# Second expert layer: 24 of 32 experts in the order of their rows, with 32 slots each, four at a time

## The chip, the cores and the metric

The kernel runs on one core of a Trainium2 chip. The metric is the device time of one execution in microseconds (us); each time given for a kernel is the median of several runs. The profile is of one execution.

## The reference

Two transformer blocks work one after the other on 256 tokens of width 1024; each ends in a mixture of experts. The change lies in the second one, `hier_moe`, in 32-bit floats:

```python
def hier_moe(h, w_rg, b_rg, w_re, b_re, w1e, w3e, w2e):
    t = h.reshape(-1, d)                                   # 256 x 1024
    pg = softmax(t @ w_rg + b_rg)                          # 4 groups
    pg_top, g_idx = top_k(pg, 1)
    le = (t @ w_re + b_re).reshape(-1, 4, 8)               # 8 experts of each group
    le_sel = take_along_axis(le, g_idx[:, :, None], axis=1)[:, 0]
    pe_top, e_idx = top_k(softmax(le_sel), 2)
    wts = pg_top * pe_top / sum(pe_top)
    cw = ...                                               # 256 x 32, two weights in each row
    for e in range(32):
        he = silu(t @ w1e[e]) * (t @ w3e[e])               # 1024 -> 256
        out = out + cw[:, e:e + 1] * (he @ w2e[e])         # 256 -> 1024
    return out
```

Each token goes to two experts of one group, so 512 rows are spread over 32 experts, 16 for each on average, and unevenly. The expert layer of the first block has 32 experts too, with larger weights and four experts for each token.

## The kernel before, in words

`Ker.run` calls four stages: `block1`, `moe1` (first expert layer), `block2`, `moe2` (second expert layer, the end of the kernel). A scheduler places each instruction on its engine's queue, by the order of the program and by what is ready at that point; an engine then works its queue in order.

In `moe2` every expert has 64 slots. `slots` ranks the tokens of each expert with matrix products and gives `pm`, the slot of each token in each expert (-1 where it isn't routed there), and the counts. `onehots` (L1152) makes the selection matrices `oh` of four experts, `gather` (L1207) multiplies the tokens with them, so that `g` holds the 256 slots of four experts side by side, and hands out its steps as a generator that `first2` draws from. `first2` (L1435) takes two experts: for gate weights `w1e` and then up weights `w3e`, eight steps of 128 rows, both experts in turn, each with 64 of the 128 columns of the array (L1445, tile `ab`). `second2` (L1453) is a generator in three parts: transposes (L1456, L1458) and the requests for the down weights `w2e`; down products (L1471, tile `y`) and their weighting by the router (`weighted`, L1176 and L1177); and eight products that add the rows back to the tokens (L1478, tile `sum`). `step2` moves each pending `second2` one part further; it is called between the gate and the up products of `first2` and after it. So the down products of a pair come after the up products of the pair behind it, and their weights are fetched before the up weights of that pair.

Weights come in tiles of 1 MB (`wload`, L302), all on SP's DMA queue: three tiles for each expert, 96 in all. They go round 13 buffers, five from the pool `wp` that all stages share (`own`) and eight from a pool of this stage (`ahead`); `fetch` asks for the next one, and the first eight tiles are asked for at the start of the stage, in the eight.

After the last expert stands `overflow` (L1226): it loads the largest count into a register of each engine (L1231), and only if an expert has more than 64 rows (L1232) it runs a loop with further slots. In `moe1` the same test stands after expert 11 of 32 (`OVF`); ahead of it the pending work is finished and the next nine tiles are requested, in the buffers of the stage's own pools alone. At the end of `moe2` the sums are gated and added to `x` (L1506, L1507), normed and stored.

The modulation rows (`modrow`, L358, tile `modps`) are products with 32 stationary columns, four side by side in the array.

Of the kernel before, what the change touches and what calls it, by code (L numbers as in the profile page):

```python
# [15 lines left out]
PSUM = bass.MemoryType.PSUM  # L16

# [3 lines left out]
OVF = 11  # L21
MODS1 = [(1, j) for j in range(4, 12)] + [(2, j) for j in range(12)]
# [50 lines left out]
def shape_consts():  # L73
    c = {}
    ident = np.eye(128, dtype=np.float32)
    perm = np.zeros((128, 128), np.float32)
    for m in range(128):
        b, r = divmod(m, 64)
        perm[b * 64 + (r + 32) % 64, m] = 1.0
    tri = (np.arange(128)[:, None] < np.arange(128)[None, :]).astype(np.float32)  # L80
    n_freq = 16
    inv = (np.float32(10000.0) ** (-np.arange(n_freq, dtype=np.float32) / np.float32(n_freq))).astype(np.float32)
    row = np.repeat(np.arange(4), 64).astype(np.float32)
    col = np.tile(np.arange(64), 4).astype(np.float32)
# [6 lines left out]
    c['fconst'] = np.ascontiguousarray(np.concatenate([ident, fold, tri, iota, perm, cosT, sinT], 1))  # L91
# [139 lines left out]
class Ker:  # L231
# [296 lines left out]
    def block1(self, p, late, xtile):  # L528
# [24 lines left out]
        nc.sync.dma_start(rc, d['fconst'][:, 544:])  # L553
# [427 lines left out]
        ys = {}  # L981
# [150 lines left out]
    def slots(self, p, sel):  # L1132
# [12 lines left out]
        cnt = p.tile([128, 33], I32, name="cnt")  # L1145
        nc.vector.tensor_copy(cnt[:, 0:32], ps[:, 64:96])
        mx = self.sm.tile([128, 1], F32, name="cmax")
        nc.vector.reduce_max(mx, ps[:, 64:96], axis=AX.X)
        nc.vector.tensor_copy(cnt[:, 32:33], mx)  # L1149
        return pm, cnt  # L1150

    def onehots(self, p, pm, e0):  # L1152

        nc = self.nc
        oh = p.tile([128, 2, 4, 64], F32R, name="oh", tag="oh", bufs=2)
        for b in range(2):
            nc.vector.tensor_tensor(oh[:, b], self.iota[:, None, 0:64].to_broadcast([128, 4, 64]),
                                    pm[:, b, e0:e0 + 4, None].to_broadcast([128, 4, 64]), op=OP.is_equal)
        return oh
# [66 lines left out]
    def overflow(self, p, cnt, pm, cw, xs, A, B, expert, gbufs=1):  # L1226
# [4 lines left out]
        most = nc.values_load(cnt[0:1, 32:33], min_val=0, max_val=256)  # L1231
        with tc.If(most > 64):  # L1232
            with tc.For_i(0, 32) as i:
                n = nc.values_load(cnt[0:1, bass.ds(i, 1)], min_val=0, max_val=256)
                with tc.If(n > 64):
# [3 lines left out]
                    for r in range(1, 4):  # L1239
# [9 lines left out]
                        expert(g, 0, i, ohv, w)  # L1249
# [48 lines left out]
    def moe1(self, p, route, ahead, spare):  # L1298
# [24 lines left out]
        pm, cnt = self.slots(p, sel)  # L1323
# [19 lines left out]
        for e in range(32):  # L1343
# [19 lines left out]
            if e == OVF:  # L1363
# [4 lines left out]
                self.overflow(p, cnt, pm, cw, xs, A, B, late)  # L1368
# [3 lines left out]
    def moe2(self, p, route, ahead):  # L1372
# [8 lines left out]
        def fetch(n, e, slot=None):  # L1381
            if isinstance(e, int) and (n, e) in first:
                return first.pop((n, e))
            return self.wload(src(n, e), slot=slot)
        first = {}
        first = {k: fetch(*k, ahead) for k in [(n, e) for e0 in (0, 2) for n in ('w1e', 'w3e', 'w2e') for e in (e0, e0 + 1)][:NW2B]}
        self.wi = 0

        gs = self.rp.tile([128, 1024], F32, name="gsb", tag="gf")
# [7 lines left out]
        pm, cnt = self.slots(p, sel)  # L1397
# [37 lines left out]
        def first2(g, c0, e0, feed):  # L1435
            ps = self.ps("ab")
            for i, n in enumerate(('w1e', 'w3e')):
                if i:
                    step2()
                w = [fetch(n, e0 + j).rearrange("p (k n) -> p k n", k=8) for j in range(2)]  # L1440
# [12 lines left out]
        def second2(act, e0, oh, wv):  # L1453
# [3 lines left out]
            for b in range(2):  # L1457
                nc.tensor.transpose(pt[:, 256 + 128 * b:384 + 128 * b],  # L1458
                                    oh[:, b, e0 % 4:e0 % 4 + 2, :].bitcast(F32).rearrange("p e s -> p (e s)"), self.ident)
# [4 lines left out]
            w2 = [fetch('w2e', e0 + j) for j in range(2)]  # L1464
            yield
            ys = []
            for s in range(2):
                y = self.ps("y")
                for k in range(2):
                    for j in range(2):  # L1470
                        nc.tensor.matmul(y[64 * j:64 * j + 64, :], aT[:, 128 * k + 64 * j:128 * k + 64 * j + 64],  # L1471
# [3 lines left out]
            for b in range(2):  # L1475
                for s in range(2):
                    for i in range(2):
                        nc.tensor.matmul(sums[b][s], oT[:, 128 * b:128 * b + 128], ys[s][i], start=(e0 + i == 0), stop=(e0 + i == 31))  # L1478

        for e in range(0, 32, 2):  # L1480
            if e % 4 == 0:
                oh = self.onehots(p, pm, e)
                g, feed = self.gather(p, xs, 4, [oh[:, b].rearrange("p e s -> p (e s)") for b in range(2)], A, B, 2)
                next(feed)
            if e == 16:
                self.bcast_rows([(3, 2), (3, 3)], [gs[:, c] for c in cs],
                                lambda o, ps: nc.vector.scalar_tensor_tensor(o, ps, 1.0, o, op0=OP.add, op1=OP.mult))
            act = first2(g, 64 * (e % 4), e, feed)
            if e == 0:
                cw = cw()  # L1490
            if e % 4 == 0:
                sw = self.slot_weights(p, [(slice(64 * (j % 2), 64 * (j % 2) + 64), j // 2, [oh[:, b, j, :] for b in range(2)],
                                            [cw[:, b, e + j:e + j + 1] for b in range(2)]) for j in range(4)], "sw", 2)
            step2()
            pend.append(second2(act, e, oh, sw[:, e // 2 % 2:e // 2 % 2 + 1]))
        while pend:
            step2()
        self.overflow(p, cnt, pm, cw, xs, A, B, late, 2)
# [631 lines left out]
```

## Time and profile before

| | |
|---|---|
| time, median of 3 runs | 2146.15 us (2144.57 to 2146.51) |
| time of the profiled execution | 2146.77 us |
| its span, first to last instruction | 2144.9 us |
| PE busy in the span | 2007.6 us (94%) |
| mean granted TensorE clock | 0.970 of full |
| moved by DMA | 646.08 MB, 301 GB/s on the mean |
| second expert layer, first gather to last sum | 1842 to 2123 us |

PE is TensorE's matrix products, PEld its weight loads, DVE VectorE, ACT ScalarE, POOL GpSimd, SP SyncE, whose queue issues the weight transfers; a "q" behind an engine's name means its sequencer. Products on PE are pipelined and their ends are modelled, so that a busy PE isn't PE at its peak. A line like L1445 is a line of the kernel, `out<-in` the tiles written and read, `128*64 128x512` a product with 64 stationary columns and 512 moving ones. Each 32-bit product shows as two instructions; products of tiles split into a high and a low part show as one. In brackets stands the idle time before an instruction, and what ended it.

### The profile page before, as it was taken

The page shows a single profiled execution, that of the slowest core. Times are in us where ns is not written, and L with a number is a line of the kernel's source. Part 1 is how long each engine was busy: PE and PEld are TensorE (multiplying, and loading weights), DVE is VectorE, ACT ScalarE, POOL GpSimd, SP SyncE. Part 2 cuts the span into 40 slices and gives each one's busy share as a digit, 9 for nine tenths or more (in the row PEclk, how much of TensorE's full clock was granted, in tenths as well). Part 3 has the DMA queues.
Part 4 walks back from the last instruction along what each step waited for, and adds up shares of the span by engine and source line. Part 5 has one row for each costly group of instructions (what it writes and reads, how often), then busy time and mean ns, then how long its engine had stood idle before and what let it go on. Part 6 is the DMA issues. An engine that isn't in the chain of part 4 may idle for free. (4 is left out here: it accounts for less than half of the span.)

```text
span 2144.9 us, 30936 instructions
## 1 busy us (share of the span) xinstructions
PE 2007.6 (94%) x13008; PEld 1172.9 (55%) x13009; DVE 918.6 (43%) x1766; ACT 529.8 (25%) x927; POOL 63.2 (3%) x66
## 2 busy tenths in 40 slices
PE   5999999999899999989999999999789998899995
PEld 3788888877633333333333333333268997665552
DVE  5766664454323332332423333333477654322223
ACT  3434463444300000000000000010244634312112
POOL 0000000000000000000000000000033101000000
PEclk9999999999999999989999999999899998999998
DMA  9254637622899999889999999999662232799980
GB/s 356 83 228 184 234 128 282 247 90 82 325 426 427 412 427 417 366 360 405 427 427 427 426 427 427 426 427 427 243 239 105 100 135 105 316 387 381 358 337 26
DMA packets 95127, 646.08 MB, mean 301 GB/s; under 512 B 11524, under 2 KB 12548, under 8 KB 19076
## 3 DMA queue, kind: packets, MB, share of 16 engines
q1 hardware_dynamic: 93296, 642.79, 74.0%
q8 instruction: 107, 1.75, 0.3%
q10 hardware_dynamic: 1684, 1.21, 0.2%
q14 instruction: 40, 0.33, 0.0%
HBM read 642.91 MB, written 1.05 MB: 300 GB/s over the span
## 5 line engine op out<-in xcount | busy, mean ns | idle before, releaser
L1262 PE MATMUL gu<-w,gT 128*64 128x512 f32 x2048 | 480.9, 596 | 0.0
L1262 PEld LDWEIGHTS gu<-w,gT 128*64 128x64 f32 x2048 | 148.1, 137 | 277.7 <-issue 255.8
L1293 PE MATMUL y<-w,aT 128*64 128x512 f32 x1024 | 231.0, 604 | 0.4
L487 DVE TENSOR_TENSOR wsl<-w,wsh 128x1024 fp32r<-128x1024 f32 (+1 forms) x141 | 168.5, 1205 | 98.5 <-ACT wsh L486 98.3
L486 ACT CAST wsh<-w 128x1024 fp32r<-128x1024 f32 (+1 forms) x141 | 143.4, 1030 | 167.0 <-PE tp L500 109.2
L1272 DVE TENSOR_SCALAR act<-gu 128x256 f32<-128x256 f32 x64 | 27.2, 424 | 307.2 <-PE gu L1332 303.9
L1177 DVE SCALAR_TENSOR_TENSOR ylo<-y,sw,yhi 128x512 fp32r<-128x512 f32 x64 | 48.1, 751 | 254.7 <-ACT yhi L1176 254.7
L1293 PEld LDWEIGHTS y<-w,aT 128*64 128x64 f32 x1024 | 72.5, 140 | 149.7 <-issue 143.4
L499 PE MATMUL tp<-hs,wsh 128*128 128x256 f32 (+1 forms) x424 | 140.2, 331 | 0.0
L501 PE MATMUL tp<-hs,wsl 128*128 128x256 f32 (+1 forms) x424 | 134.9, 318 | 4.1 <-DVE wsl L487 4.1
L500 PE MATMUL tp<-hs,wsh 128*128 128x256 f32 (+1 forms) x424 | 134.2, 317 | 0.0
L1445 PE MATMUL ab<-w,gT 128*64 128x256 f32 x1024 | 128.0, 383 | 0.1
L1176 ACT ACTIVATE yhi<-y,sw 128x512 fp32r<-128x512 f32 x64 | 44.0, 687 | 294.9 <-PE y L1332 241.9
L1193 DVE TENSOR_TENSOR gated<-co,gtb 128x512 f32<-128x512 f32 x128 | 88.3, 690 | 34.9 <-PE co L1188 27.4
L1274 ACT ACTIVATE sge<-act 128x512 f32<-128x512 f32 x32 | 20.2, 630 | 331.3 <-DVE act L1272 331.3
L1445 PEld LDWEIGHTS ab<-w,gT 128*64 128x64 f32 x1024 | 77.9, 137 | 39.6 <-issue 10.7
L499 PEld LDWEIGHTS tp<-hs,wsh 128*128 128x128 f32 x424 | 82.4, 194 | 16.3 <-issue 4.9
L1218 PE MATMUL ga<-oh,xhi 128*128 128x256 f32 x256 | 75.8, 325 | 15.9 <-DVE cnt L1149 6.9
L1194 DVE TENSOR_TENSOR x<-x,gated 128x512 f32<-128x512 f32 x128 | 88.2, 689 | 3.3
L501 PEld LDWEIGHTS tp<-hs,wsl 128*128 128x128 f32 x424 | 82.2, 194 | 9.8 <-DVE wsl L487 4.7
L499 PE MATMUL tp<-hi,wsh 128*128 128x256 f32 x288 | 85.5, 297 | 0.0
L500 PEld LDWEIGHTS tp<-hs,wsh 128*128 128x128 f32 x424 | 82.3, 194 | 4.5 <-issue 0.7
(548 smaller groups left out, 3242.1 us busy)
## 6 DMA issues: line engine op xcount, KB each, us to landing
w<-in_wgu_dram SPq DMA_DIRECT2D x256, 1024.0 KB, 13.4
w<-in_wdn_dram SPq DMA_DIRECT2D x128, 1024.0 KB, 14.1
w<-in_win_dram SPq DMA_DIRECT2D x50, 1024.0 KB, 5.8
w<-in_w3e_dram SPq DMA_DIRECT2D x32, 1024.0 KB, 8.8
w<-in_w1e_dram SPq DMA_DIRECT2D x32, 1024.0 KB, 9.2
w<-in_w2e_dram SPq DMA_DIRECT2D x32, 1024.0 KB, 7.6
w<-in_wada_dram SPq DMA_DIRECT2D x24, 1024.0 KB, 6.0
w<-in_wmod_dram SPq DMA_DIRECT2D x16, 1024.0 KB, 5.7
```

The lines of the kernel that those rows point to most:

```text
L486: nc.scalar.copy(hi, src)
L487: nc.vector.tensor_sub(lo, src, hi.bitcast(F32))
L499: nc.tensor.matmul(out, a[0], b[0], start=first, stop=False)
L500: nc.tensor.matmul(out, a[0], b[1], start=False, stop=False)
L501: nc.tensor.matmul(out, a[1], b[0], start=False, stop=last)
L1177: nc.vector.scalar_tensor_tensor(lo, y, w, hi.bitcast(F32), op0=OP.mult, op1=OP.subtract)
L1193: nc.vector.tensor_mul(part, o[s], gate[:, cs])
L1194: nc.vector.tensor_add(x[:, b, cs], x[:, b, cs], part)
L1218: nc.tensor.matmul(ps[:, 256 * kk:256 * kk + 64 * n], xs[i][:, b, 128 * (k + kk):128 * (k + kk) + 128], ohv[b], start=(b + i == 0), stop=( ...
L1262: nc.tensor.matmul(gu[j][64 * s:64 * s + 64, :], g[:, k, c0:c0 + 64], w[:, 1024 * s + 512 * j:1024 * s + 512 * j + 512], start=(k == 0), s ...
L1293: nc.tensor.matmul(y[64 * s:64 * s + 64, :], aT[:, k % 4, k // 4, :], w[:, o:o + 512], start=(k == 0), stop=False)
L1445: nc.tensor.matmul(ps[64 * j:64 * j + 64, 256 * i:256 * i + 256], g[:, k, c0 + 64 * j:c0 + 64 * j + 64], w[j][:, k, :], start=(k == 0), st ...
```

## The change

The experts of `moe2` get places. Experts 0 to 3 keep theirs (`FIXED`); the other 28 are sorted by their number of rows, most first, on the chip (`sorted_places`): a key from the count, a comparison of all keys with each other, a permutation matrix `perm`, and the table `inv` of the expert at each place. `by_place` permutes the slots and the router weights (`pmP`, `cwP`) with transposes and products.

Places 0 to 7 (`WIDE`) have 64 slots and go two at a time as before; places 8 to 31 have 32 slots and go four at a time, each with 32 of the 128 columns, and a gather serves eight experts instead of four. From place 4 on SP loads the expert's number from `inv` into a register (`place`), and the address of its weights is worked out from it. The order of requests, the 13 buffers and the number of tiles stay.

The overflow test, which now asks whether a count exceeds the slots of its place, moves from the end of the stage to the point behind place 15: the pending halves are finished there, and eight tiles (gate and up weights of places 16 to 19) are requested in the stage's own eight buffers. `moe1` gets the new form of the test with its 64 slots. The table `fconst` grows by 97 columns, which ACT's queue loads at the start of `moe2`.

```diff
+FIXED, WIDE = 4, 8
...
+    off = np.zeros((128, 97), np.float32)
+    e = np.arange(32)
+    off[:, 0:32] = np.where(e < FIXED, 32768 * (FIXED - e), -e)
+    off[0:32, 32] = off[0, 0:32]
+    off[:, 33:65] = np.where(e < WIDE, 64, 32)
+    off[0:32, 65:97] = e[:, None]
+    c['fconst'] = np.ascontiguousarray(np.concatenate([ident, fold, tri, iota, off, perm, cosT, sinT], 1))
...
+    def excess(self, p, over):
+        nc = self.nc
+        exc = p.tile([128, 33], I32, name="exc")
+        nc.vector.tensor_copy(exc[:, 0:32], over)
         mx = self.sm.tile([128, 1], F32, name="cmax")
+        nc.vector.reduce_max(mx, over, axis=AX.X)
+        nc.vector.tensor_copy(exc[:, 32:33], mx)
+        return exc
+
+    def sorted_places(self, p, sel, pm, count, off):
         nc = self.nc
+        keyrow, keycol, self.caps, ecol = off[:, 0:32], off[0:32, 32:33], off[:, 33:65], off[0:32, 65:97]
+        key = p.tile([128, 32], F32, name="key")
+        nc.vector.scalar_tensor_tensor(key, count, 64.0, keyrow, op0=OP.mult, op1=OP.add)
+        pc = self.ps("kc")
+            nc.tensor.matmul(pc[0:32, 0:1], sel[:, b, :], self.ones[:, 0:1], start=(b == 0), stop=(b == 1))
+        kcol = p.tile([32, 2], F32, name="kcol")
+        nc.vector.scalar_tensor_tensor(kcol[:, 0:1], pc[0:32, 0:1], 64.0, keycol, op0=OP.mult, op1=OP.add)
+        gt = p.tile([32, 64], F32, name="gt")
+        nc.vector.tensor_scalar(gt[:, 0:32], key[0:32, :], kcol[:, 0:1], None, op0=OP.is_gt)
+        nc.vector.reduce_sum(kcol[:, 1:2], gt[:, 0:32], axis=AX.X)
+        perm = gt[:, 32:64]
+        nc.vector.tensor_scalar(perm, self.iota[0:32, 0:32], kcol[:, 1:2], None, op0=OP.is_equal)
+        pi = self.ps("inv")
+        nc.tensor.matmul(pi[0:32, 0:32], ecol, perm, start=True, stop=True)
+        inv = p.tile([32, 32], I32, name="inv")
+        nc.vector.tensor_copy(inv, pi[0:32, 0:32])
+        pmP = self.by_place(p, pm, perm, "pmP")
+        cc = p.tile([32, 128], F32, name="cc")
+        nc.vector.tensor_copy(cc, pc[0:32, 0:1].to_broadcast([32, 128]))
+        po = self.ps("cp")
+        nc.tensor.matmul(po[:, 0:32], cc, perm, start=True, stop=True)
+        over = p.tile([128, 32], F32, name="over")
+        nc.vector.tensor_sub(over, po[:, 0:32], self.caps)
+        return perm, inv, pmP, self.excess(p, over)
+
+    def by_place(self, p, t, perm, name):
+        nc = self.nc
+        pt = self.ps("plT")
+        for b in range(2):
+            nc.tensor.transpose(pt[0:32, 128 * b:128 * b + 128], t[:, b, :], self.ident)
+        tT = p.tile([32, 256], F32, name="plT")
+        nc.scalar.copy(tT, pt[0:32, 0:256])
+        po = self.ps("pl")
+        for b in range(2):
+            nc.tensor.matmul(po[:, 32 * b:32 * b + 32], tT[:, 128 * b:128 * b + 128], perm, start=True, stop=True)
+        o = p.tile([128, 2, 32], F32, name=name)
+        nc.vector.tensor_copy(o.rearrange("p b e -> p (b e)"), po[:, 0:64])
+        return o
...
-        with tc.If(most > 64):
+        with tc.If(most > 0):
...
+        def place(q):
+            if q >= FIXED and q not in expert:
+                expert[q] = nc.values_load(inv[0:1, q:q + 1], engines=(SP,), min_val=0, max_val=31)
+
+        def request(names):
+            for n, q in names[:NW2B]:
+                place(q)
+                first[n, q] = fetch(n, q, ahead)
+        request([(n, e) for e0 in range(0, FIXED, 2) for n in ('w1e', 'w3e', 'w2e') for e in (e0, e0 + 1)])
         self.wi = 0
...
-        def first2(g, c0, e0, feed):
+        def first2(g, c0, es, feed):
+            m = 128 // len(es)
...
+                w = [fetch(n, e).rearrange("p (k n) -> p k n", k=8) for e in es]
...
-                    for j in range(2):
-                        nc.tensor.matmul(ps[64 * j:64 * j + 64, 256 * i:256 * i + 256], g[:, k, c0 + 64 * j:c0 + 64 * j + 64], w[j][:, k, :],
+                    for j in range(len(es)):
+                        nc.tensor.matmul(ps[m * j:m * j + m, 256 * i:256 * i + 256], g[:, k, c0 + m * j:c0 + m * j + m], w[j][:, k, :],
...
+        blocks = [(e, 4, e < FIXED) for e in range(0, WIDE, 4)] + [(e, 8, False) for e in range(WIDE, 32, 8)]
+        for e0, n, fixed in blocks:
+            oh = self.onehots(p, pm if fixed else pmP, e0, n)
...
+            m = n // 2
+            for h in range(2):
+                es = range(e0 + m * h, e0 + m * h + m)
+                for q in es:
+                    place(q)
+                act = first2(g, 128 * h, es, feed)
+                if e0 == h == 0:
+                    cw = cw()
+                    perm, inv, pmP, exc = self.sorted_places(p, sel, pm, count, off)
+                    cwP = self.by_place(p, cw, perm, "cwP")
...
+                step2()
+                ohv = [oh[:, b].rearrange("p e s -> p (e s)")[:, 128 * h:128 * h + 128] for b in range(2)]
+                pend.append(second2(act, es, ohv, sw[:, h:h + 1], e0 + h == 0, e0 + n == 32 and h == 1))
+            if e0 == WIDE:
+                while pend:
+                    step2()
+                request([(n_, q) for n_ in ('w1e', 'w3e') for q in range(e0 + n, e0 + n + 4)])
+                self.overflow(p, exc, self.caps, pmP, cwP, xs, A, B, late, 2, inv)
         while pend:
             step2()
-        self.overflow(p, cnt, pm, cw, xs, A, B, late, 2)
```

## Rows read from the trace of the kernel before

**Rows 1.** Windows, second expert layer: start:end, length, busy of engines, PEclk, DMA share, GB/s.
```profile
1835.00:1840.00 5.00, 3.11 (x15) 1.72 (x14) 3.67 (x32) 4.57 (x12) 0.00 (x0) 1.00 0.82 283
1840.00:1915.00 75.00, 71.66 (x549) 50.09 (x549) 22.88 (x62) 15.62 (x31) 0.00 (x0) 0.98 0.98 408
1915.00:2000.00 85.00, 83.53 (x556) 50.15 (x555) 21.35 (x43) 15.59 (x29) 0.00 (x0) 1.00 0.93 376
2000.00:2092.00 92.00, 89.06 (x606) 52.19 (x604) 22.00 (x45) 17.93 (x33) 0.00 (x0) 1.00 0.90 344
2092.00:2095.00 3.00, 3.00 (x15) 1.37 (x16) 0.75 (x1) 0.31 (x1) 0.00 (x0) 1.00 0.01 3
```

**Rows 2.** Waits of SP's queue, 1795 to 2145: total us, times, longest us.
```profile
SPq L302 <- PE ab L1445: 145.9, 26, 12.4
SPq L302 <- PE y L1471: 63.6, 18, 9.2
```

**Rows 3.** Timeline of SP's queue: the first requests of the layer.
```profile
1772.19 21.65 SPq L302 DMA_DIRECT2D w<-in_w3e_dram  x2
1802.03 9.59 SPq L302 DMA_DIRECT2D w<-in_w1e_dram  x2
1818.28 0.33 SPq L302 DMA_DIRECT2D w<-in_w2e_dram  x1
1835.05 0.80 SPq L302 DMA_DIRECT2D w<-in_w1e_dram  x2
```

**Rows 4.** Timeline of PE, several places: start, length, instruction, count.
```profile
53.61 1.93 PE L358 MATMUL modps<-wmx,cpad 128*32 128x256 f32 x32
...
1540.88 3.64 PE L358 MATMUL modps<-w,cpad 128*32 128x512 f32 x32 [0.32 <-DVE gated L1193]
...
1842.44 0.55 PE L1218 MATMUL ga<-oh,xhi 128*128 128x256 f32 x1 [3.43 <-DVE cnt L1149]
...
1869.11 0.39 PE L1218 MATMUL ga<-oh,xhi 128*128 128x256 f32 x1
...
1878.64 0.39 PE L1478 MATMUL sum<-ylo,oT 128*128 128x512 f32 x1
...
1878.87 0.40 PE L1478 MATMUL sum<-yhi,oT 128*128 128x512 f32 x1
...
1879.86 3.67 PE L1445 MATMUL ab<-w,gT 128*64 128x256 f32 x32
...
1900.40 0.39 PE L1218 MATMUL ga<-oh,xhi 128*128 128x256 f32 x1
...
1933.38 0.28 PE L1218 MATMUL ga<-oh,xhi 128*128 128x256 f32 x1
...
1933.50 0.28 PE L1218 MATMUL ga<-oh,xlo 128*128 128x256 f32 x1
...
2116.54 3.65 PE L1471 MATMUL y<-w,aT 128*64 128x512 f32 x16 [0.52 <-DVE aT L1461]
```

**Rows 5.** Windows, first expert layer, around its overflow test and behind it.
```profile
900.00:920.00 20.00, 18.36 (x84) 6.08 (x82) 6.15 (x11) 1.90 (x3) 0.00 (x0) 0.93 0.43 174
938.00:944.00 6.00, 4.79 (x20) 3.98 (x22) 1.45 (x3) 1.13 (x2) 0.00 (x0) 0.50 0.47 143
...
990.00:1500.00 510.00, 496.60 (x2449) 177.63 (x2446) 173.25 (x302) 41.28 (x67) 0.00 (x0) 0.99 1.01 427
```

**Rows 6.** Instructions of L1231 and L1232: count, ns min/median/max, first and last start.
```profile
L1231 SPq TENSOR_LOAD <-cnt x2: 287/382/478, 929.8 to 2088.1; - x2
...
L1232 SPq EVENT_SEMAPHORE  x9: 17/17/17, 936.2 to 939.9; - x9
...
L1232 SPq COMPARE_BRANCH  x1: 45/45/45, 930.4 to 930.4; - x1
...
L1232 PEldq COMPARE_BRANCH  x2: 3807/4910/6014, 932.6 to 2122.2; - x2
```

**Rows 7.** Timeline, end of the layer.
```profile
2121.83 0.73 PE L1478 MATMUL sum<-ylo,oT 128*128 128x512 f32 x2
...
2126.20 1.29 DVE L1506 TENSOR_TENSOR xo<-sum,gtb 128x512 f32<-128x512 f32 x2 [4.42 <-PEq L1232]
```

More of the change, by code (lines that the diff above doesn't have):

```diff
@@ L1159, in onehots @@
+    def onehots(self, p, pm, e0, n=4):
+        nc = self.nc
+        m = 256 // n
+        oh = p.tile([128, 2, 256], F32R, name="oh", tag="oh", bufs=2).rearrange("p b (e s) -> p b e s", e=n)
+        for b in range(2):
+            nc.vector.tensor_tensor(oh[:, b], self.iota[:, None, 0:m].to_broadcast([128, n, m]),
+                                    pm[:, b, e0:e0 + n, None].to_broadcast([128, n, m]), op=OP.is_equal)
         return oh
@@ L1224, in gather, with overflow @@
         return g, steps()
-    def overflow(self, p, cnt, pm, cw, xs, A, B, expert, gbufs=1):
+    def overflow(self, p, exc, caps, pm, cw, xs, A, B, expert, gbufs=1, inv=None):
         nc, tc = self.nc, self.tc
@@ L1238, in overflow @@
                     nc.vector.tensor_copy(pc[:, :, 1:2], cw[:, :, bass.ds(i, 1)])
-                    for r in range(1, 4):
+                    cap = p.tile([128, 1], F32, name="ocap")
+                    nc.vector.tensor_copy(cap, caps[:, bass.ds(i, 1)])
+                    for b in range(2):
+                        nc.vector.tensor_sub(pc[:, b, 0:1], pc[:, b, 0:1], cap)
+                    for r in range(4):
                         oo = p.tile([128, 2, 64], F32R, name="oo")
@@ L1248, in overflow @@
                             pass
-                        expert(g, 0, i, ohv, w)
+                        expert(g, 0, e, ohv, w)
         self.last_sig, self.wq, self.wi = sig, wq, 0
@@ L1322, in moe1 @@
         xs = self.split_tokens(p, x, r)
-        pm, cnt = self.slots(p, sel)
+        pm, count = self.slots(p, sel)
+        caps = p.tile([128, 32], F32, name="caps")
+        nc.vector.memset(caps, 64.0)
+        over = p.tile([128, 32], F32, name="over")
+        nc.vector.tensor_sub(over, count, caps)
+        exc = self.excess(p, over)
         def wl(e):
@@ L1367, in moe1 @@
                 first = {(e + 1, j): fetch(e + 1, j, spare if j < NW2X else ahead) for j in range(NW2 + NW2X)}
-                self.overflow(p, cnt, pm, cw, xs, A, B, late)
+                self.overflow(p, exc, caps, pm, cw, xs, A, B, late)
         pend()
@@ L1379, in src, with fetch @@
             return d[n][e] if isinstance(e, int) else d[n][bass.ds(e, 1)].rearrange("e k n -> (e k) n")
[L1381 to L1386, printed above, removed]
+        first, expert = {}, {}
+        def fetch(n, q, slot=None):
+            if isinstance(q, int) and (n, q) in first:
+                return first.pop((n, q))
+            return self.wload(src(n, expert.get(q, q) if isinstance(q, int) else q), slot=slot)
+        def place(q):
[6 more added lines that the diff above has]
+        request([(n, e) for e0 in range(0, FIXED, 2) for n in ('w1e', 'w3e', 'w2e') for e in (e0, e0 + 1)])
         self.wi = 0
+        off = p.tile([128, 97], F32, name="off")
+        nc.scalar.dma_start(off, d['fconst'][:, 544:641])
         gs = self.rp.tile([128, 1024], F32, name="gsb", tag="gf")
@@ L1396, in moe2 @@
         xs = self.split_tokens(p, x, r)
-        pm, cnt = self.slots(p, sel)
+        pm, count = self.slots(p, sel)
         def late(g, c0, e, ohv, w):
@@ L1451, in first2, with second2 @@
             return act
-        def second2(act, e0, oh, wv):
+        def second2(act, es, ohv, wv, begin, end):
+            m = 128 // len(es)
             pt = self.ps("aT")
@@ L1463, in second2 @@
             nc.scalar.copy(oT, pt[:, 256:])
-            w2 = [fetch('w2e', e0 + j) for j in range(2)]
+            w2 = [fetch('w2e', e) for e in es]
             yield
@@ L1469, in second2 @@
                 for k in range(2):
[L1470 to L1471 removed]
+                    for j in range(len(es)):
+                        nc.tensor.matmul(y[m * j:m * j + m, :], aT[:, 128 * k + m * j:128 * k + m * j + m],
                                          w2[j][:, 1024 * k + 512 * s:1024 * k + 512 * s + 512], start=(k == 0), stop=(k == 1))
@@ L1477, in second2 @@
                     for i in range(2):
[L1478 to L1485, printed above, removed]
+                        nc.tensor.matmul(sums[b][s], oT[:, 128 * b:128 * b + 128], ys[s][i], start=(begin and i == 0), stop=(end and i == 1))
@@ L1486, in moe2 @@
+        blocks = [(e, 4, e < FIXED) for e in range(0, WIDE, 4)] + [(e, 8, False) for e in range(WIDE, 32, 8)]
+        for e0, n, fixed in blocks:
+            oh = self.onehots(p, pm if fixed else pmP, e0, n)
+            g, feed = self.gather(p, xs, 4, [oh[:, b].rearrange("p e s -> p (e s)") for b in range(2)], A, B, 2)
+            next(feed)
+            if e0 == 16:
                 self.bcast_rows([(3, 2), (3, 3)], [gs[:, c] for c in cs],
                                 lambda o, ps: nc.vector.scalar_tensor_tensor(o, ps, 1.0, o, op0=OP.add, op1=OP.mult))
-            act = first2(g, 64 * (e % 4), e, feed)
```

37 lines of the change are left out of this document (13 added, 24 removed).

## Prediction

> **What bounds the kernel now.** I read the page first (PE busy 94% of the span, granted clock 0.97 of full), then the windows of the second expert layer, the waits of SP's queue, and the timelines of PE and SP there. In [rows 1] the reader is to see a queue that is fast at first and then slackens: 408 GB/s, 376, 344, and nothing after 2092. What it carries from 1835 to 2092 is 283 x 5 + 408 x 75 + 376 x 85 + 344 x 92 = 95.6 MB, 91 tiles of 1.049 MB; the layer has 96, and five had been issued earlier [rows 3]. The queue had more to give: 427 GB/s over 510 us of the first layer [rows 5]. It slackens because SP waits for buffers: 145.9 us in total for the gate and up products and 63.6 us for the down products [rows 2]. So PE sets the pace of the second layer, and 30 us of its work lie behind the last landing (2092 to the last sum, which begins at 2121.83 and ends at 2122.56 [rows 7]). The end is a serial chain on DVE and ACT from 2126.20 to 2144.9. The first layer, whose queue is full nearly all the time, gets a few small DVE operations (0.4 us at most) and is left as it is.
>
> **What PE saves.** PE runs two 64-column products side by side: 32 instructions of 256 columns in 3.67 us. At 32 columns the trace has the modulation rows, four side by side with four different right-hand sides: 32 instructions in 1.93 us, and 32 of 512 columns in 3.64 us where 16 down products take 3.65 us [rows 4]. So four experts at 32 slots cost what two cost at 64. For a half block of four experts: gate 3.9, up 3.9, down 3.65, eight sums at 0.23 each 1.8, transposes 0.6; the gather is 32 instructions at 0.12, 3.7 us, and the slot weights about 1.2, once for the block of eight. A block: 2 x 13.9 + 4.9 = 32.5 us of PE for eight experts, where the old blocks of four follow each other at 31.3 us (1869.11 to 1900.40) [rows 4]. The 24 narrow experts need 3 x 32.5 = 98 us of PE.
>
> **What takes over.** Their 72 tiles need, at 421 GB/s (the first layer's 427, less a little because single stretches of this layer lie near 420; the difference is 3 us in all), 72 x 2.49 = 179 us of the queue. PE then waits for weights, and the time is that of the queue: its start, its volume, its holes, and the work behind its last tile.
>
> Volume. The eight fixed requests go out at 1835.05 as now, and by 1840 the queue has moved 1.35 tiles [rows 1, 3]. Five early tiles become fewer, since two of them (the gate weights of experts 4 and 5, issued from 1802.03) now need an address that doesn't exist yet: the up weights of experts 2 and 3 surely stay early, the down weights of 2 and 3 perhaps. Two to four; I take three. Left at 1840: 96 - 3 - 1.35 = 91.65 tiles, 228.2 us, so 2068.2 without a hole.
>
> Hole at the start. The eight fixed tiles last until about 1857. The sorting needs the selection (there before 1842.44, when the gather starts) and some ten small DVE and PE operations in a row; if they fill gaps the addresses are ready by 1850, if they stand behind the first half block they come near 1860, and a register load adds 0.3 to 0.5 us [rows 6]. Behind SP's wait stand all later weights. 0 to 8 us, taken 3. On PE the new transposes and products are hidden, once the layer is bound by the queue, by the wait for weights; without that cover they cost 2 to 3 us.
>
> Buffers in the 64-slot part. Blocks 0 to 7 run as now, and there the queue loses 75 x (1 - 408/421) = 2.3 us [rows 1]. By 1901 they are done.
>
> The overflow test in the middle. Now it lies at the end of the layer, where PE's branch takes 3.8 us and DVE waits 4.4 us for it [rows 6, 7]; from the last sum to the first DVE operation that is 3.6 us, all of it saved. The place for what it costs in the middle is the first layer's test, at 930 [rows 5, 6]. SP branches at 930.4, and its semaphore waits run from 936.2 to 939.9, until everything on order has landed; the queue runs dry and moves 143 GB/s over 938 to 944, a loss of 6 x (1 - 143/427) = 4.0 us. PE's branch of 6.0 us is covered, as PE has 60 us of queue for each 32.5 us of work. Before that test stands another hole: over 900 to 920 the queue moved 174 GB/s, 20 x (1 - 174/427) = 11.8 us lost, because the prefetch may use only the spare buffers and waits for those that the last down products hold. The new code drains and prefetches in the same way. Followed through the buffers here, the first request waits for the down weights of expert place 11, read some 10 us after the up weights of 12 to 15 have landed; meanwhile the four down tiles of 12 to 15 keep the queue busy for 10 us. The hole is 2 to 3 us, if PE keeps time. Together 4 to 15.8 us, taken 7.
>
> Buffers in the 32-slot part. Tiles go in fours through 13 buffers, and the down weights are held longest: they land 10 us before the up weights fetched after them, then come 3.9 us of up and 3.65 us of down products. The queue then has about two tiles of slack, or none if PE is slow off the mark. 0 to 6 us in all, taken 2.
>
> Last landing: 2068.2 + 3 + 2.3 + 7 + 2 = 2082.5. Behind it the last four down tiles wait for the preceding half's down products, sums and transposes (about 3 us), then go the same 6.0 us from 2116.54 to 2122.56 as now [rows 4, 7]: 9 us (6 to 13). Then 0.2 us to DVE and the chain of 18.7 us, 2110.4 as span, and the 1.9 us that the profiled time lies above its span: **2112 us**. That profiled time, 2146.77, is 0.6 above the median of 2146.15, less than I can resolve.
>
> The register loads themselves: 28 of about 0.5 us, and a few register operations for each address, on an SP that otherwise waits for buffers for over 200 us [rows 2]. Nothing, as long as SP takes less than 2.49 us a tile.
>
> **Rivals.**
>
> [...]
>
> *A thin queue: slower than before.* With fours of tiles and requests that wait for a register or a buffer, few may be on order at once. In the last stretch before, where each request waits for a buffer, the rate is 344 GB/s, 3.05 us a tile [rows 1]. For the 84 register-addressed tiles that is 84 x 0.56 = 47 us more: 2159. It decides from 2112 to 2146, 34/84 = 0.41 us a tile, that is 2.90 us or 362 GB/s. The same price stands if an address from a register slows a transfer, of which no row here says anything. Against it: in that stretch PE frees buffers too late, in the new one it frees them in fours and early. [...]
>
> *No overlap of four.* If 32-column products didn't run four at a time, gate, up and down would cost double: 2 x 25.4 + 4.9 = 56 us a block, 167 in all, still below 179; with late buffers perhaps 2117 us. [rows 4] speak against it.
>
> *The overflow loop runs.* Then the change doesn't do what it says. Counting the choices of the reference's router on its own inputs gives at most 49 rows for an expert, and from the ninth place on at most 21, below 32: the branch isn't taken.
>
> **How the numbers follow.** Forecast 0.70 (2096 to 2137 by adding up the bounds, the low one also with 427 GB/s), half clock 0.12 at 2128, no overlap 0.05 at 2117, thin queue 0.09 at 2159, everything given back elsewhere, near 2146, 0.04. A measurement of this kernel can tell 0.2%, 4 us. Faster 0.89, same 0.03, slower 0.08. The range 2096 to 2135 leaves out the thin queue, the case of no gain, and the edges of the forecast.
>
> **What would show it.** Right: a queue share near 1 from block 8 on, at about 420 GB/s, with one hole at the test; last landing near 2082 and the last sum within 10 us of it; PE idle on weights; 64 instructions of 32 columns in 3.9 us. Wrong: a queue below 380 GB/s in the narrow part (thin queue); clock 0.5 with PE busy throughout (half clock); SP waiting for the address table past 1860; a hole near 12 us ahead of the test.

## The result, and the profile after

The changed kernel takes 2109.95 us, the median of 4 runs (2107.76 to 2111.07), against 2145.59 us of the kernel before in the same series (4 runs): a ratio of 0.9831, 95% interval 0.9818 to 0.9844. In a second series the ratio was 0.9838 (0.9823 to 0.9853; run "again" below). The forecast was 2112, with a range of 2096 to 2135.

The windows of the second expert layer, the view of [rows 1], in the profiled execution (2111.07 us, span 2109.3):

```profile
1835.00:1840.00 5.00, 2.54 (x16) 2.02 (x16) 3.63 (x9) 3.00 (x10) 0.00 (x0) 0.94 1.02 426
1840.00:1860.00 20.00, 18.98 (x107) 11.62 (x107) 6.95 (x34) 4.65 (x8) 0.00 (x0) 0.76 0.70 294
1860.00:1974.00 114.00, 100.41 (x797) 57.39 (x798) 24.47 (x51) 17.51 (x32) 0.00 (x0) 0.94 1.01 419
1974.00:1986.00 12.00, 10.93 (x184) 6.89 (x182) 3.00 (x7) 2.08 (x4) 0.00 (x0) 1.00 0.46 160
1986.00:2084.00 98.00, 75.97 (x596) 31.22 (x594) 10.88 (x21) 9.04 (x17) 0.00 (x0) 0.91 0.99 416
2084.00:2095.00 11.00, 6.02 (x31) 2.13 (x28) 6.55 (x12) 4.15 (x11) 0.00 (x0) 0.86 0.00 0
```

The last number of each line is the queue's rate. Where the kernel before went from 408 to 376 to 344 GB/s, this one stays between 416 and 426, except in two holes: one behind 1854 (294 over the 20 us, 6.1 us lost against 424) and one at the overflow test (160 over 12 us, 7.5 us lost). PE, busy in 71.66 + 83.53 + 89.06 = 244 of the 252 us from 1840 to 2092 in [rows 1], is now busy in 76 of the 98 us behind the test. The waits of SP's queue, the view of [rows 2], say the same:

```profile
SPq L311 <- PE ab L1529: 40.3, 9, 8.2
SPq L311 <- PE y L1555: 26.5, 8, 8.1
SPq L1461 <- DVE inv L1185: 21.2, 1, 21.2
SPq L1292 <- SPq L1292: 15.9, 2, 15.4
```

145.9 and 63.6 us for buffers have become 40.3 and 26.5; new are 21.2 us for the table of addresses (`inv`) and 15.9 us inside the overflow test. What is left of the waits for buffers lies ahead of the test. Behind it, from 1980 to 2100, SP waits for something else, namely until an earlier transfer of its own queue has landed:

```profile
SPq L311 <- DMA w<-in_w1e_dram: 21.4, 11, 2.2
SPq L311 <- DMA w<-in_w2e_dram: 19.5, 10, 2.6
SPq L311 <- DMA w<-in_w3e_dram: 15.6, 8, 2.0
...
SPq L311 <- PE ab L1529: 0.4, 1, 0.4
SPq L311 <- PE y L1555: 0.4, 1, 0.4
```

That is 56.5 us for its own transfers and 0.8 us for buffers: there the queue is held up by hardly anything but itself. The kernel before has 0.7 us of such waits for a transfer from 1795 to 2145. The first requests of the layer, as in [rows 3]:

```profile
1832.44 0.81 SPq L311 DMA_DIRECT2D w<-in_w1e_dram  x2
1833.34 1.07 SPq L311 DMA_DIRECT2D w<-in_w3e_dram  x2
1834.46 0.98 SPq L311 DMA_DIRECT2D w<-in_w2e_dram  x2
1835.54 24.38 SPq L311 DMA_DIRECT2D w<-in_w1e_dram  x4
```

Of the four gate weights that begin at 1835.54 the last two need an address from the table, and the line lasts 24 us for it. The start of the layer varies by some 3 us from one execution to another, with the same code ahead of it. So two measures are used from here on: the median, and the length of the layer in one profile, from its first request (1832.44 here) to the end of the span. The kernel before: 2144.9 - 1835.05 = 309.9. The changed one: 2109.3 - 1832.44 = 276.9, and 273.7 in its second profile.

The end, PE's timeline, answering to [rows 4] and [rows 7]:

```profile
2074.16 5.33 PE L1529 MATMUL ab<-w,gT 128*32 128x256 f32 x58 [1.87 <-DMA w<-in_w3e_dram]
...
2082.11 5.54 PE L1555 MATMUL y<-w,aT 128*32 128x512 f32 x32 [0.52 <-DVE aT L1545]
...
2089.29 0.73 PE L1562 MATMUL sum<-ylo,oT 128*128 128x512 f32 x2
```

PE waits for the last up weights until 2074.16, the queue is empty at 2084, and the last sum ends at 2090.0. The end of the layer now hangs on the queue, but for the 5.33 us of the up products, which took 3.64 us in the second profile (below).

### The profile page after: what moved, and what is told of

The parts are those of the page before. It is cut to its first block, busy times and chain, and to the rows that moved or that the text cites. A ratio compares the mean times of both kernels' runs of the same rounds, so it can differ in the third digit from the quotient of the medians.

```text
span 2109.3 us, 30791 instructions
## 1 busy us (share of the span) xinstructions
PE 1945.5 (92%) x12860; PEld 1114.6 (53%) x12861; DVE 896.0 (42%) x1727; ACT 511.6 (24%) x893; POOL 63.3 (3%) x66
## 5 line engine op out<-in xcount | busy, mean ns | idle before, releaser
L1237 DVE SCALAR_TENSOR_TENSOR ylo<-y,sw,yhi 128x512 fp32r<-128x512 f32 x52 | 39.0, 751 | 264.5 <-ACT yhi L1236 264.0
L1529 PE MATMUL ab<-w,gT 128*32 128x256 f32 (+1 forms) x1024 | 99.8, 415 | 17.4 <-DMA w<-in_w1e_dram 10.8
L1236 ACT ACTIVATE yhi<-y,sw 128x512 fp32r<-128x512 f32 x52 | 35.8, 688 | 300.9 <-PE y L1402 239.9
L1278 PE MATMUL ga<-oh,xhi 128*128 128x256 f32 x208 | 63.5, 333 | 21.9 <-PEq L1292 6.3
L509 PE MATMUL tp<-lo,wsh 128*128 128x256 f32 x288 | 81.7, 284 | 0.0
## 6 DMA issues: line engine op xcount, KB each, us to landing
w<-in_w2e_dram SPq DMA_DIRECT2D x32, 1024.0 KB, 15.9
```

Source lines behind the costliest of these rows:

```text
L509: nc.tensor.matmul(out, a[0], b[1], start=False, stop=False)
L1237: nc.vector.scalar_tensor_tensor(lo, y, w, hi.bitcast(F32), op0=OP.mult, op1=OP.subtract)
L1278: nc.tensor.matmul(ps[:, 256 * kk:256 * kk + 64 * n], xs[i][:, b, 128 * (k + kk):128 * (k + kk) + 128], ohv[b], start=(b + i == 0), stop=( ...
L1529: nc.tensor.matmul(ps[m * j:m * j + m, 256 * i:256 * i + 256], g[:, k, c0 + m * j:c0 + m * j + m], w[j][:, k, :], start=(k == 0), stop=(k ...
```

## The experiments

All start from the changed kernel, called "base" here: median 2109.95 in one series and 2109.15 in another. Where several edits are alike, one diff stands for them. The experiments fall into three series. The kernel before took 2143.9 us in that of "test at the end", "sort first" and the two with more fixed addresses, and 2147.2 and 2147.3 us in the two others, so between series the ratios to the kernel before are to be compared, not the times. A length of the layer comes from one profile, and the two profiles of the base differ by 3.2 us; a difference of 2 to 3 us in the layer is therefore no more than this noise, unless the trace shows where it lies.

**Again: the base unedited.**

> The changed kernel once more, unedited, as the base of the others on this chip. The layer, from the first fixed request to the end of the execution, took 276.9 us in its first profile. If that is the kernel's usual layer, it is 275 to 279 again. If a part of it belonged to that one execution (the last 64 gate and up products ran 5.3 us at half clock there, 3.6 us in three of the experiments before), it is 273 to 275.

Measured: 2109.15 us (2108.53 to 2112.18); layer 273.7 (1833.08 to 2106.8). So 3 us of the first profile's layer belonged to that execution. This profile is the base for layers below. Its two holes, its last up products and its last down products:

```profile
1854.00:1862.00 8.00, 6.86 (x52) 4.27 (x48) 2.87 (x13) 1.11 (x3) 0.00 (x0) 0.80 0.53 185
1862.00:1972.00 110.00, 96.64 (x767) 54.46 (x767) 23.13 (x46) 17.51 (x32) 0.00 (x0) 0.95 1.01 422
1972.00:1982.00 10.00, 10.00 (x141) 6.41 (x143) 2.45 (x5) 1.69 (x3) 0.00 (x0) 1.00 0.37 135
1982.00:2080.00 98.00, 75.49 (x647) 31.48 (x636) 11.84 (x24) 9.43 (x18) 0.00 (x0) 0.93 1.01 422
```
```profile
2071.52 3.64 PE L1529 MATMUL ab<-w,gT 128*32 128x256 f32 x58 [1.86 <-DMA w<-in_w3e_dram]
...
2081.48 3.62 PE L1555 MATMUL y<-w,aT 128*32 128x512 f32 x20 [0.52 <-DMA w<-in_w2e_dram]
```

Lost at the start 8 x (1 - 185/424) = 4.5 us, at the test 10 x (1 - 135/424) = 6.8. The 58 products that took 5.33 us in the first profile, at a granted clock of 0.68 of full, take 3.64 here at the full clock (1.00 over 2070 to 2080), and the last down products wait for the queue.

**Test at the end.**

```
-            if e0 == WIDE:
-                while pend: step2()
-                request([...w1e, w3e of places 16 to 19...])
-                self.overflow(...)
         while pend:
             step2()
+        self.overflow(p, exc, self.caps, pmP, cwP, xs, A, B, late, 2, inv)
```

> The overflow test goes back to the end of the layer; nothing else changes. Theory (the weight queue sets the end, each of its holes counts in full): the hole of about 7.5 us between 1974 and 1984 goes, the branch after the last sum comes back with 3.6 us: about 4 us less than the changed kernel, 2106 us (2104 to 2108), the queue at about 424 GB/s right through 1960 to 2060, last landing near 2076. Rival (the drain is hidden, PE sets the end, or the lost time comes back as a wait for buffers): 3.6 us more, 2113.5 us.

Measured: 2106.29 us (ratio to the kernel before 0.9817, 0.9799 to 0.9834); layer 270.2, 3.5 less than the base. The window view of this kernel:

```profile
1840.00:1860.00 20.00, 19.04 (x131) 12.31 (x129) 7.95 (x38) 4.64 (x8) 0.00 (x0) 0.84 0.80 326
1860.00:2066.00 206.00, 182.91 (x1506) 91.95 (x1508) 36.30 (x72) 27.83 (x51) 0.00 (x0) 0.95 1.01 424
```

One rate, 424 GB/s over 206 us, and the hole at the start as before. The last four requests begin 214.7 us after the first instead of 221.2, and the end comes 55.5 us behind them instead of 52.5. The theory holds: the hole at the test is gone, and the rival's 2113.5 is excluded. The size of the gain, 3.5 us, rests on the profiles; the ratios to the kernel before (0.9838 and 0.9831 for the base) have intervals that overlap.

**Sort first.** Its operations are issued before the gate products of experts 0 and 1 instead of behind them.

```
             next(feed)
+            if e0 == 0:
+                perm, inv, pmP, exc = self.sorted_places(p, sel, pm, count, off)
...
                 if e0 == h == 0:
                     cw = cw()
-                    perm, inv, pmP, exc = self.sorted_places(p, sel, pm, count, off)
```

> The sort's operations are issued before the gate products of the first half block instead of behind them; nothing else changes. Theory (the address table comes late because its two products stand in PE's queue behind the gate and up products of experts 0 and 1, and the queue runs dry for it): the table is there before 1850, no stretch at 0 GB/s between 1854 and 1862, PE starts its gate products 3 to 6 us later, which costs nothing, and the time is 6 us less than the changed kernel: 2104 us (2102 to 2106). Rival 1 (the time lost there is made up later, at a buffer wait): 2110 us. Rival 2 (PE's delay in the first blocks moves all that follows, since buffers come free later): 2112 to 2115 us.

Measured: 2107.09 us (ratio 0.9823, 0.9808 to 0.9839); layer 270.9, 2.8 less than the base. PE's timeline, first of the base as first profiled, then of this kernel:

```profile
1853.39 0.29 PE L1174 MATMUL kc<-ones,sel 128*32 128x1 f32 x4
1857.21 0.24 PE L1183 MATMUL inv<-gt,off 32*32 32x32 f32 x2
```
```profile
1838.33 0.32 PE L1174 MATMUL kc<-ones,sel 128*32 128x1 f32 x4
...
1842.04 0.31 PE L1183 MATMUL inv<-gt,off 32*32 32x32 f32 x2
```

The table comes 15 us earlier, and the queue moves 424 GB/s over 1840 to 1860: the cause of the hole is shown. But only 2.8 of its 4.5 us are won, since the queue then drops to 397 GB/s over 1900 to 1920 (1.3 us): it is ahead, and waits for buffers. My 6 us came from the first profile. By the time alone, the gain is not clear of noise, since the ratio lies inside the base's interval (0.9823 to 0.9853).

**Eight fixed addresses; all addresses fixed.** `FIXED = 8`, and `FIXED = 32`, in place of 4.

> The first eight experts keep their fixed addresses and only the places from 8 on are sorted; the test stays in the middle. Theory (queue): the hole of 6 us at 1855 to 1861 goes, since the first address is wanted 12 tiles later, and the five early tiles are back instead of three, 2 x 2.49 = 5 us: 11 us less than the changed kernel, 2099 us (2097 to 2102). Rival 1 (the early tiles are worth nothing, for the queue waits for buffers of the 64-slot part anyway): 2104 us. Rival 2 (both are eaten later): 2110 us.

> All 32 experts stay in their own order with fixed addresses, 8 with 64 slots and 24 with 32; the sort's operations are still carried out, but no weight load takes its address from a register (on these inputs no expert from 8 on has over 24 rows). Theory (an address in a register costs the queue nothing): the same as with eight fixed places, 2099 us, within 1.5 us of it. Rival (a register address slows a transfer or SP): less by 0.1 us or more for each of 72 tiles, 2092 us or below.

Measured: 2106.89 us (ratio 0.9823, 0.9807 to 0.9839) and layer 271.2 with eight (2.5 less than the base, within the noise); 2104.07 us (0.9807, 0.9791 to 0.9822) and layer 268.6 with all fixed, another 2.6 less. With eight, the hole at 1855 is gone and five tiles are early instead of two, yet most of it is given back at once:

```profile
1860.00:1880.00 20.00, 19.48 (x130) 12.50 (x130) 4.31 (x8) 3.83 (x7) 0.00 (x0) 0.88 0.74 295
1880.00:1900.00 20.00, 20.00 (x157) 13.51 (x158) 4.47 (x10) 3.07 (x6) 0.00 (x0) 1.00 0.85 340
```

SP waits 13.4 us in one go for gate and up products there: 6.1 + 4.0 us lost. In the 64-slot part PE sets the pace (busy in 39.5 of these 40 us), and a queue that is ahead of it with 13 buffers has nothing to do. That is the mechanism of rival 1; the time lies between those of the two rivals.

That all-fixed gains 2.6 us on eight-fixed fits neither of the two sentences; the place is seen at the test. SP's instructions there, in the base: its waits in the test (the last at 1976.0), the address loads, the first request:

```profile
L1292 SPq EVENT_SEMAPHORE  x9: 17/17/17, 1960.5 to 1976.0; - x9
...
L1461 SPq TENSOR_LOAD <-inv x4: 263/269/275, 1976.3 to 1978.1; - x4
L1461 SPq FUSED_REGOPS  x4: 147/147/155, 1976.7 to 1978.4; - x4
L1461 SPq SEQ_ASSERT  x4: 18/18/18, 1976.9 to 1978.6; - x4
```
```profile
1978.92 3.03 SPq L311 DMA_DIRECT2D w<-in_w1e_dram  x4
```

and with all addresses fixed:

```profile
L1292 SPq EVENT_SEMAPHORE  x9: 17/17/17, 1960.5 to 1975.9; - x9
...
1976.36 2.16 SPq L311 DMA_DIRECT2D w<-in_w1e_dram  x4
```

From the last wait to the first request 2.9 us in one case, 0.46 in the other. Four addresses cost SP about 0.6 us each, and here the queue is dry while it loads them. Elsewhere they are hidden: with the test at the end the queue ran at 424 GB/s over 206 us, addresses from registers nearly all along.

**Scale rows later.** The broadcast products that stood in PE's queue behind the test (`if e0 == 16:`) are moved to `if e0 == 24:`.

> The four broadcast products of the final scale rows (2.8 to 3.6 us of PE) move from behind the overflow test to the last block; nothing else changes. Behind the test the next request waited for gate products of places 16 to 19, which stand behind these products on PE, while everything on order had landed 2 us before. Theory (PE's chain behind its branch sets the restart of the queue): the hole is 2 to 3 us shorter, 2106.5 us. Rival (the drain of SP sets it, and PE is covered there): no change, 2109 to 2110 us.

Measured: 2108.97 us, layer 274.3: no change. PE began the gate products at 1971.46 instead of 1973.20, but SP's last wait ended at 1976.5, the four address loads took until 1979.1, and the request left at 1979.47. My theory was wrong: SP's drain (its waits until everything on order has landed) and its address loads set the restart, and PE is covered there.

**Both: sort first and test at the end.** The two diffs above together; then the same with nine buffers for the tiles ahead (`NW2B = 9`).

> Both edits together: the sort's operations before the first gate products, and the overflow test at the end of the layer. In the profiles so far the layer took 276.9 us with neither, 270.9 with the first alone, 270.2 with the second alone. Theory (one queue, holes add up): 264 to 265 us of layer, 2098 us in all. Rival (the queue, once it is ahead, waits for buffers that PE frees in the 64-slot part, as with eight fixed places): 268 to 270 us of layer, 2103 us.

> The sort first and the test at the end (2102.1 us), with nine instead of eight buffers for the weights ahead, 14 in all. Theory (what is left of holes, 409 and 395 GB/s over 1880 to 1920, are waits for buffers): 1.5 to 2 us less, 2100 us. Rival (they have another cause): 2102 us.

Measured: 2102.11 us (2101.40 to 2103.35), ratio 0.9800 (0.9786 to 0.9814), layer 266.8. This is faster than the base in the same series (0.9838, 0.9823 to 0.9853) beyond both intervals, which neither edit alone is, and the fastest version here that does the whole work. Counted from the base's second profile the two edits add up, 273.7 - 2.8 - 3.5 = 267.4; the 264 to 265 of the theory started from the longer first profile, and the rival's 268 to 270 is passed. In time, 2102.1 is nearer to the rival's 2103 than to the theory's 2098, and a part of the rival is there: SP's waits over 1875 to 1925 are all for buffers (18.3 us for gate and up products, 15.2 for down products). What that leaves of holes is 40 x (1 - 402/424) = 2 us:

```profile
1840.00:1880.00 40.00, 37.23 (x261) 25.55 (x263) 13.53 (x47) 8.53 (x16) 0.00 (x0) 0.87 1.01 424
1880.00:1920.00 40.00, 39.31 (x331) 24.64 (x329) 10.14 (x22) 7.36 (x14) 0.00 (x0) 1.00 0.98 402
1920.00:2070.00 150.00, 125.34 (x1080) 55.48 (x1076) 22.52 (x43) 16.92 (x31) 0.00 (x0) 0.95 1.01 424
```

With nine: 2105.01 us (2100.45 to 2105.70), ratio 0.9799, layer 268.0: no change. Its queue is full from 1840 on, 424 GB/s over 1880 to 1920 too, so the small hole is gone. But the ninth request at the start of the layer is an up weight that went out by 1793 with eight buffers, and now goes out at 1840.13; one early tile (2.5 us) is lost for the 2 us won. A queue that is 2.5 us later would find more buffers free in any case, so this run doesn't separate the ninth buffer from the lost tile.

**PE's work doubled; bytes halved.**

```
-                for k in range(8):
+                for k in [*range(8)] * (len(es) // 2):
```
```
+            if isinstance(q, int) and q >= WIDE and n != 'w2e':
+                return self.wload(a[:, 0:1024], 1024, slot=slot)
...
-  ... w[j][:, k, :], ...
+  ... w[j][:, k % 4 if len(es) == 4 else k, :], ...
```

> In the 32-slot part every gate and up product is done twice (the second pass starts the sum afresh, so the result is the same): 6 half blocks x 2 x 3.7 to 4 us = 45 to 48 us more of PE's work, not one byte more. Theory (PE has about 80 us of slack there, and only the last pair and some buffers are late): 0 to 12 us more than the changed kernel, 2114 us. Rival (PE's pace, or its half clock, sets the time): 40 us or more, 2150 to 2157 us.

> In the 32-slot part only the first half of each gate and up weight is loaded, and used twice, so the output isn't the reference's; PE's instructions are the same. 48 tiles of half the size are 24 tiles less, 24 x 2.49 = 60 us of the queue. Theory (the bytes set the time; PE's 98 us for the part lie below the 120 us that are left): 52 to 60 us less than the changed kernel, about 2054 us. Rival (PE with its bursts at half clock, or the number of requests, is close behind): 2070 us or more.

Measured: with PE's products doubled 2117.75 us (2115.76 to 2120.03), ratio 0.9873 (0.9855 to 0.9891), layer 282.0; with the bytes halved 2074.80 us (2073.57 to 2075.74), ratio 0.9661 (0.9646 to 0.9677), layer 238.4. PE's timeline, one batch of products in the base (second profile) and then one of the doubled kernel:

```profile
1926.49 3.66 PE L1529 MATMUL ab<-w,gT 128*32 128x256 f32 x64
```
```profile
1932.40 7.11 PE L1529 MATMUL ab<-w,gT 128*32 128x256 f32 x128
```

Doubling costs 3.45 us a batch, 12 x 3.45 = 41 us of PE in all, not the 45 to 48 of the expectation. This run is inside what the theory allowed: of 41 us of more PE work 8.6 show, and over 2000 to 2080 the queue still moves 423 GB/s. The second is the rival's: of 60 us of less queue only 34 to 35 are won. Behind the test PE is then full, and the queue nearly so, in the window view of the kernel with half the bytes:

```profile
1980.00:2040.00 60.00, 56.96 (x640) 28.38 (x632) 10.98 (x22) 8.67 (x16) 0.00 (x0) 1.00 1.01 406
```

From its first narrow gate product (1916.6) to its last sum (2054.7) PE waits for weights for only 1.3 us there, so PE sets the pace of that run. The two runs put PE's slack in the 32-slot part at 33 to 35 us, not at the 80 of the prediction.

**The sort alone.** All 32 places with 64 slots (`WIDE = 32`), test at the end; then the same with the sort first.

> The sort, the addresses in registers and the change of order alone: all 32 places keep 64 slots and go two at a time, the test is at the end. Theory (the gain is that of PE's work in fours; without it PE is the bound again and has slack for a 6 us hole of the queue at the start): the time of the kernel before, 2144 to 2148 us. Rival (a part of the gain comes from how the requests go out, or from the order): 2135 us or less.

> As with all 32 places at 64 slots in sorted order (2161 us), but with the sort's operations before the first gate products, so that the address table is early. Theory (most of the 14 us lost there is PE's wait for weights that were ordered late): 8 to 10 us less, 2152 us. Rival (it is the sort's own work on PE and the two engines' exchange, or the addresses in registers): 2158 to 2162 us, or more, as PE now waits for the exchange.

Measured: 2161.42 us, ratio 1.0070 (1.0051 to 1.0090), and 2157.36 us, 1.0043 (1.0027 to 1.0059). For the first both sentences were wrong: with PE as the bound the sort costs 14 us. It is seen on PE: from the first gather to that of the second block it takes 26.7 us in [rows 4] (1842.44 to 1869.11), 38.7 here (1840.24 to 1878.89), 33.4 with the sort first (1839.99 to 1873.40). The window views of these three stretches, in the same order:

```profile
1842.44:1869.11 26.67, 25.77 (x197) 19.27 (x197) 7.97 (x30) 5.36 (x9) 0.00 (x0) 0.94 1.01 420
```
```profile
1840.24:1878.89 38.65, 35.82 (x216) 21.97 (x217) 12.23 (x44) 6.67 (x16) 0.00 (x0) 0.78 0.85 350
```
```profile
1839.99:1873.40 33.41, 30.79 (x217) 20.29 (x217) 12.00 (x44) 6.61 (x15) 0.00 (x0) 0.85 1.01 424
```

Of the 12 us in this block the early table takes back 5, and 7 stay, so for the second run the rival was nearer. What neither sentence names is the granted clock (the number before the last two): 0.94, 0.78 and 0.85 of full. Against a full clock that is a loss of 1.6, 8.5 and 5.0 us (1 less the clock, times 26.67, 38.65 and 33.41), so by this estimate the lower clock makes up about 7 of the 12 us, and about half of the 7 that stay; the sort's own work and exchange have the rest. Why the granted clock is lower in these two runs was not tested. Nor was a further part: blocks 2 to 4 together take 7.9 us longer than before in both runs.

## Why the prediction was right, point by point

**The bound.** Right. PE's pace gave way to the queue's, and the queue gives 424 GB/s (421 taken; 1.6 us less in all). The waits for buffers fell as expected; the edits that closed a hole of the queue shortened the layer, together by 6.9 us; 41 us more of PE's work cost 8.6; and behind the test SP waited for its own transfers and hardly for buffers.

**Volume.** Right for two errors that cancel: two early tiles instead of three (the down weights of experts 2 and 3 are requested behind the gate weights of 4 and 5, and waited for the table with them), and a start 2 to 2.6 us earlier, in the part of the kernel that is the same. The second is luck: over all profiles the first request goes out between 1832.2 and 1835.6. With 92 GB/s over 1830 to 1835 and 426 over the next five, 2.6 MB or 2.5 tiles had moved by 1840, so 96 - 2 - 2.5 = 91.5 were left, against 91.65.

**Holes.** The sum was 3 + 2.3 + 7 + 2 = 14.3; the base's profiles show 6.1 and 4.5 at the start, 1.3 and 0.5 from there to the test, 7.5 and 6.8 at the test, 1.8 and 0.5 behind it: 16.7 and 12.3 in all. The sum was about right, and its parts were off; that they cancel is luck. The start was mis-sized: the table stood behind the first half block, the late one of my two cases, and that half block ran in part at half clock (0.50 of full over 1840 to 1848 of the first profile; 0.76 and 0.84 on the mean of 1840 to 1860 in the two). The 2 us for buffers in the 32-slot part did not come: behind the test SP waited 0.8 us for them. The 2.3 us for buffers did not come on top, since a queue that has lost time at the start finds its buffers free; the same two terms change places when the sort comes first or eight addresses are fixed. By these runs they should have been one term, the larger of the two.

**The test.** 7 us was right, by other parts than mine. The hole ahead of it, which I took from 900 to 920 in [rows 5], isn't there: the requests went out in time. The drain is longer than the 4.0 us of the first layer, because four address loads stand between it and the next request: 2.4 of the 6.8 us. So the step "the register loads cost nothing" failed at this one place, where its cover, a queue with work, is gone.

**Behind the last landing.** 9 us taken, 6.0 measured (2084.0 to 2090.0): PE had done the preceding half's work by then. In exchange the end from the first `xo` took 20.2 us instead of 18.7; 1.3 of it lie behind the issue of the output stores, see below.

**PE's need.** 98 us was too little: the runs with doubled products and halved bytes leave PE 33 to 35 us of slack, and in the second of them PE takes 138 us for the part. Left out were its waits for DVE before the transposes and the down products (7.5 us in that run), its branch (6.8 us), and a granted clock below full (0.95 on the mean, by estimate some 6.6 of the 138 us); what makes up the rest was not broken down. It did no harm, as the queue was still the longer of the two, but it is the term that would have failed had the change cut bytes as well.

**Rivals.** Half clock came in patches only, and did not set the time: 41 us more of PE's work cost 8.6. The granted clock was 0.56 of full over 1967 to 1972 of the second profile, after PE's stop at the branch, and full over 1972 to 1982. Waits for weights had either outcome in that profile: the clock was 0.55 over 1984 to 1994, where PE waited 1.4 to 1.7 us for one gate weight after another, and full over 2036 to 2048 and 2066 to 2075, with waits of 0.3 and 1.9 us for up weights.

```profile
1984.00:1994.00 10.00, 4.86 (x26) 1.34 (x30) 0.33 (x1) 0.00 (x0) 0.00 (x0) 0.55 1.01 426
```

So waits for weights went with the lower clock over 1984 to 1994 and not over the other two; what decides it, no run shows. Nor does a run show the half clock through the whole 32-slot part that the 2128 stands for: over 1982 to 2080 of the second profile the clock was 0.93 of full on the mean. The thin queue is refuted: fours of tiles with register addresses ran at 424 GB/s over 1920 to 2070 in the run with the sort first and the test at the end. The four products side by side overlap: 58 instructions of 32 columns in 3.64 us. The loop in the test was not entered.

What the change is worth by parts: the sort alone costs 14 us, and the 32 slots in fours give about 54 on top of it (ratios 1.0070 and 0.9817, with the test at the end in both). The test's place costs 3.5 us and the sort's place 2.8 by one profile each, neither clear of noise in the times; both mended give 2102.1, which is.

## What to carry to other kernels

A transfer queue that sets the end can turn a stop of its issuing engine into time (here 2.9 us from SP's last wait in the test to its next request, 0.46 without the address loads), unless it would have waited for buffers later anyway, so look for what stands between that engine's wait and its next request, address loads included, and place whatever drains it where nothing more is to be issued. Two holes of one queue are not always two terms: time lost early gives the buffers back that a queue without the loss would wait for (with eight fixed addresses the hole at 1855 went, and 10.1 us were lost to such waits over 1860 to 1900). When a change takes a bound away, work out the slack of the engine that was the bound with its waits for other engines, not from its instructions alone (here 33 to 35 us, where the instructions gave 80), since that slack was the limit of the gain from half the bytes.

## What the runs showed of the hardware that was not expected

Four address loads, with the register operations behind them, hold SP for 2.3 us (1976.3 to 1978.6 in the second profile: 0.27 us a load, 0.15 us a register operation, 0.02 us an assertion); from its last wait to its next request it is 2.9 us. From the last data on the queue to the end of SP's last wait in the test another 1 to 2 us pass: in the second profile the queue moved 45 GB/s over 1974 to 1976, and the wait ended at 1976.0:

```profile
1974.00:1976.00 2.00, 2.00 (x28) 1.43 (x24) 0.45 (x1) 0.55 (x1) 0.00 (x0) 1.00 0.11 45
1976.00:1978.00 2.00, 2.00 (x28) 1.35 (x24) 0.54 (x1) 0.41 (x2) 0.00 (x0) 1.00 0.00 0
```

From the issue of the two output stores to the end of the span it took 5.0 to 5.2 us in the kernel before and in the five experiments with the test at the end, and 5.8 to 6.4 us in the eight profiles with the test in the middle (for instance 2095.89 to 2101.0 against 2100.38 to 2106.8). The code there is the same; the cause was not found.
